# Two transpose groups per slot, and a small network's first layer moved into the runs of value products

## The chip, the cores and the metric

The kernel runs on one core of a Trainium2 chip. TensorE (PE in the profile) multiplies matrices, with its weight loads shown apart as PEld; VectorE (DVE), ScalarE (ACT) and GpSimd (POOL) work element by element; SyncE (SP) issues most of the DMA transfers. The metric is the device time of one launch in microseconds (us), the median of several runs. Before the change it is 2571.12 us (2569.76 to 2571.41 in three runs).

## The reference

Two layers on 512 rows of 1024 floats. Each layer is: a gated feed-forward block, a token mixer, a second feed-forward block, each followed by a layer norm. All time of interest here is in the token mixer:

```python
q_a, kv_a, g_a, q_b, k_b, v_b, q_c, k_c, v_c, f_c = _split_cols(h @ w_in)
o_a = _nsa(...)        # branch a: compressed + selected + window keys, gated
o_b = _swa_sink(...)   # branch b: window of 128, with a sink
o_c = _fox(...)        # branch c: causal, with a forget gate
merged = g[:, :, 0] * (o_a @ w_br_a) + g[:, :, 1] * (o_b @ w_br_b) + g[:, :, 2] * (o_c @ w_br_c)
return merged @ w_out
```

Branch a compresses its keys and values first. Blocks of 32 positions of 64 numbers, flattened to 2048, go through a small network of two layers, `gelu(flat @ w1) @ w2`, with a hidden size of 256; there is one such network for keys and one for values. The first layer, `flat @ w1`, is the "compressed branch's first layer" of this text: sixteen steps (k = 0 to 15) of 128 of the 2048 inputs each, for keys and for values.

## The kernel before, in words

**Products.** Operands of the projections are split in two halves of the fp32r type, a high and a low one (`wsplit`, lines 140 and 141: ScalarE rounds, VectorE subtracts). A product is three matmuls of 512 columns (`mm3`, lines 161 to 163: high by high, low by high, high by low).

**The fill queue.** In the mixer, a projection of 128 columns of `w_in` is a `chunk`: eight closures of three matmuls each, appended to the queue `fill`. The first closure takes the weights and a PSUM tile of the tag `mm`; the last hands the finished tile to a function that moves it out (`set_q` with `ev_q`, lines 403 and 404; `ev_k`, lines 421 and 422; `ev_z`, lines 502 to 510). `pump(n)` runs n closures. A closure wrapped in `free` counts for nothing. So the order of the chunks in the code is the order in which the projections become ready.

**Attention.** `batches` lists the work: eight pairs of branch-b units (`Swa`), then, for each of four pairs of heads, three batches of branch-c and branch-a units (`Fox`, `Nsa`). `step(cur, prev, n)` is one step of a software pipeline. It issues the score products of the batch `cur` (generator `s`: products, then bias, maximum, exponential and norm on VectorE, ScalarE and GpSimd) and the transposes of the batch `prev` (generator `tr`), spread over `slots` with closures of the fill queue between them. Then it issues the value products of `prev` (`pv`, into one PSUM tile of the tag `po`), and moves them out (line 1019). `PUMPS` has the number of closures for each step. If a batch needs a projection that isn't ready, `need` pumps until it is.

**Transposes.** One call of `next(it)` yields one group: one to four 128x128 transposes into a PSUM tile of the tag `tp` (lines 641, 692, 793, 799), which `ev_pt` copies back (line 395 on ScalarE, line 393 on VectorE). The tag has two buffers. So has `mm`; `sc`, for scores, has three, and `po` one.

**The small network.** `conv` gives eight `part` closures. Each loads two steps k of both networks into a buffer of the weights' ring `raw` (line 532, two DMAs of 256 KB) and issues four matmuls (line 536) into one PSUM tile `hid`: keys to partitions 0 to 63, values to 64 to 127. The parts are dealt out among the closures of the fill queue. After the last part comes the gelu, then `tr` (two transposes into a `tp` tile, `glT`), then `conv2`, the second layer.

**Order.** TensorE and GpSimd issue in the order of the code (`manual_schedule`); the order on VectorE, ScalarE and SyncE is made by the framework's scheduler, at build time, from its own estimate of when things are ready. PSUM and SBUF buffers of a tag are also given out at build time.

Of the kernel before, what the change touches and what calls it, by code (L numbers as in the profile page):

```python
# [18 lines left out]
P = 128  # L19
# [45 lines left out]
def body(tc, a, out, depth=DEPTH):  # L65
# [47 lines left out]
    def wraw(shape=None):  # L113
        return wt.tile(list(shape or [P, KD, P]), F32, name="raw", tag="raw", bufs=3)
# [237 lines left out]
    def mix(l, wts, pend, done_ffn, xap, xa, nxt):  # L352
# [161 lines left out]
        def conv(ws):  # L514


            c = K()
            c.wk = at.tile([P, 2, 2, DH], F32, name="cw2k", tag="p", bufs=PB)
            c.wv = at.tile([P, 2, DH], F32, name="cw2v", tag="p", bufs=PB)
            v = a["cmp_k_w2"][l].rearrange("(c p) d -> p c d", p=P)  # L520
            for r in range(2):
                nc.sync.dma_start(c.wk[:, :, r], v)
            nc.sync.dma_start(c.wv, a["cmp_v_w2"][l].rearrange("(c p) d -> p c d", p=P))
            wv = [w.rearrange("(c p) f -> p c f", p=P) for w in ws]

            def part(j):
                def go():
                    if j == 0:
                        c.p = ps("sc", "hid", (P, 256))
                    r = wraw([P, 2, 2, 256])  # L530
                    for i in range(2):
                        nc.sync.dma_start(r[:, i], wv[i][:, 2 * j:2 * j + 2])
                    for k in (2 * j, 2 * j + 1):
                        for i in range(2):
                            z = (m.zk, m.zv)[i][k // 8][:, k % 8].rearrange("p g n -> p (g n)")
                            nc.tensor.matmul(c.p[64 * i:64 * i + 64], z, r[:, i, k % 2], start=k == 0, stop=k == 15)
                    if j == 7:
                        x = at.tile([P, 2, 256], F32, name="gl", tag="p", bufs=PB)
                        t, c.t = x[:, 0], x[:, 1]
                        nc.scalar.activation(t, c.p, AF.Square)  # L540
                        nc.vector.tensor_scalar(t, t, 0.044715, 1.0, op0=OP.mult, op1=OP.add)
                        nc.vector.tensor_tensor(t, t, c.p, op=OP.mult)
                        nc.scalar.activation(t, t, AF.Tanh, scale=GELU_C)
                        nc.vector.scalar_tensor_tensor(c.t, t, 1.0, c.p, op0=OP.add, op1=OP.mult)
                return go

            def tr():
                pt = ps("tp", "glT", (P, 2, P))
                for f in range(2):
                    nc.tensor.transpose(pt[:, f], c.t[:, f * P:(f + 1) * P], ident)  # L550
                x = at.tile([P, 3, P], F32, name="glt", tag="p", bufs=PB)
                c.gk = x[:, 0].rearrange("p (f n) -> p f n", f=2)
                c.gv = x[:, 1:3].rearrange("p f (g r n) -> p f g r n", g=2, r=2)
                nc.vector.tensor_copy(c.gk, pt[:, :, 0:64])
                for f in range(2):
                    nc.vector.tensor_copy(c.gv[:, f], pt[:, f, 64:P].rearrange("p (g n) -> p g n", g=2)[:, :, None]
                                          .to_broadcast([P, 2, 2, NSLOT]))

            return c, [part(j) for j in range(8)], tr

        def conv2(c):

# [35 lines left out]
        class Swa:  # L598
# [37 lines left out]
            def tr(u):  # L636
                pv = u.p.rearrange("p s (b q) -> p s b q", q=P)[:, :, 0:u.nb]
                pt = ps("tp", "ptS", (P, 2, 2, P))[:, :, 0:u.nb]
                for s in range(2):
                    for b in range(u.nb):  # L640
                        nc.tensor.transpose(pt[:, s, b], pv[:, s, b], ident)
                ev_pt(pv, pt, 4)
                yield
# [170 lines left out]


        fill = deque()
        FREE = "free"

        def free(f):
# [5 lines left out]
        def wgf():  # L825

            r = wraw()
            v = w_in.rearrange("(k p) f -> p k f", p=P)
            nc.sync.dma_start(r[:, :, 0:24], v[:, :, CGA:CGA + 24])
            nc.sync.dma_start(r[:, :, 24:32], v[:, :, CFC:CFC + 8])  # L830
            w = wt.tile([P, KD, P], F32R, name="hi", tag="hi", bufs=3)
            nc.scalar.activation(w[:, :, 0:32], r[:, :, 0:32], AF.Copy)
            nc.vector.tensor_tensor(w[:, :, 32:64], r[:, :, 0:32], w[:, :, 0:32].bitcast(F32), op=OP.subtract)
            return w, None

        def chunk(c0, then, w=w_in, load=wcols):
            st = K()

            def part(i):
                def go():  # L840
                    if i == 0:
                        st.w = load(w, c0)
                        st.p = ps("mm", "pj")
                    proj(st.p, st.w, ks=range(i, i + 1))
                    if i == 7:
                        then(st.p)
                return go

            fill.extend(part(i) for i in range(8))

        def set_q(lst, i):
            def go(p):
                t = ev_q(p)
                fill.insert(min(4, len(fill)), free(lambda: lst.__setitem__(i, t)))
            return go
# [36 lines left out]
        def nsa_k(b):  # L892
            def go(p):
                if not m.ka:
                    for g in range(2):
                        m.ka[g] = (ks_tile(), ks_tile())
                dst = lambda g: tuple(t.rearrange("p (k b) j -> p k b j", b=2)[:, :, b] for t in m.ka[g])
                ev_k(p, dst)
            return go

        def pump(n=1):
            while n > 0 and fill:
                n -= fill.popleft()() is not FREE

# [12 lines left out]
        chunk(CKB, set_kb)  # L917
        chunk(CQB, set_q(m.qb, 0))
        chunk(0, set_gf, load=lambda w, c0: wgf())
        chunk(CQB + P, set_q(m.qb, 1))  # L920
        pump(29)
        chunk(CKV + 0, lambda p: setattr(m, "zk", ev_z(p, 0)))
        chunk(CQB + 2 * P, set_q(m.qb, 2))
        chunk(CKV + P, lambda p: setattr(m, "zv", ev_z(p, 1)))
        fill.append(lambda: m.cum())
        cv, parts, tr = conv([a["cmp_k_w1"][l], a["cmp_v_w1"][l]])
        n0 = len(fill)
        chunk(CQB + 3 * P, set_q(m.qb, 3))
        fox_chunks(0)
        rest = [fill.pop() for _ in range(len(fill) - n0)][::-1]  # L930
        for i, f in enumerate(rest):
            fill.append(f)
            if i >= 6 and parts:
                fill.append(parts.pop(0))
        fill.append(tr)
        chunk(CKV + 2 * P, nsa_k(0))
        fill.append(lambda: conv2(cv))
        chunk(CKV + 4 * P, nsa_k(1))
        chunk(CQA, set_q(m.qa, 0))
        fox_chunks(1)  # L940
        chunk(CQA + P, set_q(m.qa, 1))
        fox_chunks(2)
# [38 lines left out]
        def step(cur, prev, n):  # L981


            for u in cur:
                while not need(u):
                    pump(1)
                    n -= 1
            it, iu = chain(u.tr() for u in prev), chain(u.s() for u in cur)
            nt, ns = sum(u.ngrp for u in prev), sum(u.nseg for u in cur)
            slots = max(nt, ns, 1)  # L990
            done = 0

            def upto(x):
                nonlocal done
                x = int(round(x))
                if x > done:
                    pump(x - done)
                    done = x

            last = min(2, max(n, 0))  # L1000
            n -= last
            for j in range(slots):
                if j * ns // slots != (j + 1) * ns // slots or slots == ns:
                    next(iu, None)
                upto(n * (2 * j + 1) / (2 * slots))
                if j * nt // slots != (j + 1) * nt // slots or slots == nt:
                    next(it, None)
                upto(n * (j + 1) / slots)
            for _ in iu:
                pass  # L1010
            for _ in it:
                pass
            pump(last)
            if prev:
                po = ps("po", "po", (P, 4, P))
                for j, u in enumerate(prev):
                    u.pv(po[:, j])
                for j, u in enumerate(prev):
                    nc.scalar.activation(o_t[u.br][u.m][:, u.qb * P:(u.qb + 1) * P], po[:, j], AF.Copy)

        PUMPS = [11] * 5 + [12] * 3 + [11, 10, 11] * 4 + [8]
        for cur, prev, n in zip(batches + [[]], [[]] + batches, PUMPS):
            step(cur, prev, n)
        while fill:
# [197 lines left out]
```

## Time and profile before

| | |
|---|---|
| median of three runs | 2571.12 us (2569.76 to 2571.41) |
| the profiled execution | 2569.58 us, its span 2567.9 us |
| TensorE busy | 2549.1 us (99%) |
| VectorE, ScalarE, GpSimd busy | 1197.6, 950.1 and 177.5 us |
| granted TensorE clock, mean | 0.998 |
| attention of the first and the second layer | about 417 to 717 and 1690 to 1990 us of the span |

A row of a timeline has the start, the time from the start to the last end, the engine, the line, and what was written from what, with a count where equal neighbours are merged; a bracket holds the idle time before it and what ended it. Matmuls overlap in the pipeline: a row of 0.39 us that is followed by the next one 0.23 us later has cost 0.23 us. So prices on TensorE are read here from start to start. An fp32 matmul that is not a transpose stands in the trace as two; the transposes, and the fp32r products, as one. A row of a group has the busy time, the mean of one in ns, and after the bar the idle time of its engine before it.

### The profile page before, as it was taken

How to read it: one execution, taken by the hardware profiler on the slowest of the kernel's cores; microseconds unless marked ns; L12 is line 12 of the kernel's file. 1: busy time of each engine (PE TensorE's matmuls, PEld its weight loads, DVE VectorE, ACT ScalarE, POOL GpSimd, SP SyncE). 2: the span in 40 equal slices, each digit the busy share in tenths (PEclk: the TensorE clock that was granted, in tenths of full speed). 3: DMA queues.
4: the chain of work that ended last, by engine and by line, in shares of the span. 5: the costliest groups of instructions: out<-in, count | busy, mean ns of one | idle time of the engine just before them, and what ended most of it. 6: DMA issues, size and time to landing. Idle time of an engine off the chain costs nothing.

```text
span 2567.9 us, 34023 instructions
## 1 busy us (share of the span) xinstructions
PE 2549.1 (99%) x13099; PEld 2104.2 (82%) x13099; DVE 1197.6 (47%) x2563; ACT 950.1 (37%) x1949; POOL 177.5 (7%) x371
## 2 busy tenths in 40 slices
PE   9999999999999999999999999999999999999998
PEld 8888887788888888888888888877888888888887
DVE  4344245676654354332343432555766534544323
ACT  3222134477642332222232221345776323322211
POOL 0000000133300000000000000101332000000000
PEclk9999999999999999999999999999999999999999
DMA  6433333633143333333333333426321434233331
GB/s 214 117 93 97 99 93 112 180 91 83 50 143 99 119 102 96 99 99 93 113 91 98 93 97 99 121 77 190 90 82 41 145 101 148 81 93 98 99 93 63
DMA packets 374658, 268.97 MB, mean 105 GB/s; under 512 B 16872, under 2 KB 350760, under 8 KB 374496
## 3 DMA queue, kind: packets, MB, share of 16 engines
q1 hardware_dynamic: 373344, 262.61, 35.1%
q0 software_dynamic: 1152, 4.19, 0.4%
q8 instruction: 103, 1.69, 0.3%
q14 instruction: 59, 0.48, 0.1%
HBM read 247.83 MB, written 9.49 MB: 100 GB/s over the span
## 4 chain that ended last, share of the span: by engine, by line
PE 95%; DVE 2%; DMA 1%; ACT 1%; issue 1%; POOL 0%; DVEq 0%; POOLq 0%; ACTq 0%
PE acc L175 7%; PE acc L174 7%; PE acc L176 7%; PE pg L161 6%; PE pg L163 6%; PE pg L162 6%; PE pu L161 6%; PE pu L163 6%; PE pu L162 6%; PE pj L161 5%; PE pj L163 5%; PE pj L162 5%; PE gate L161 3%; PE gate L162 3%; PE gate L163 3%; PE brp L162 2%
## 5 line engine op out<-in xcount | busy, mean ns | idle before, releaser
L141 DVE TENSOR_TENSOR lo<-raw,hi 128x1024 fp32r<-128x1024 f32 (+2 forms) x414 | 490.8, 1189 | 856.1 <-ACT hi L140 854.5
L140 ACT ACTIVATE hi<-raw 128x1024 fp32r<-128x1024 f32 (+2 forms) x414 | 424.6, 1031 | 1225.3 <-issue 695.9
L161 PE MATMUL pj<-xh,hi 128*128 128x512 f32 (+1 forms) x720 | 272.6, 379 | 2.6 <-ACT vt L448 1.4
L163 PE MATMUL pj<-xh,lo 128*128 128x512 f32 (+1 forms) x720 | 255.5, 355 | 0.7 <-DVE lo L141 0.5
L162 PE MATMUL pj<-xl,hi 128*128 128x512 f32 (+1 forms) x720 | 254.5, 353 | 0.1
L162 PE MATMUL pg<-xl,hi 128*128 128x512 f32 x640 | 249.7, 390 | 0.0
L163 PE MATMUL pg<-xh,lo 128*128 128x512 f32 x640 | 249.7, 390 | 0.0
L161 PE MATMUL pg<-xh,hi 128*128 128x512 f32 x640 | 249.6, 390 | 0.0
L163 PE MATMUL pu<-xh,lo 128*128 128x512 f32 x640 | 249.0, 389 | 0.0
L161 PE MATMUL pu<-xh,hi 128*128 128x512 f32 x640 | 249.0, 389 | 0.0
L162 PE MATMUL pu<-xl,hi 128*128 128x512 f32 x640 | 249.0, 389 | 0.0
L174 PE MATMUL acc<-hi,ha 128*128 128x512 f32 x576 | 227.3, 395 | 0.0
L175 PE MATMUL acc<-hi,ha 128*128 128x512 f32 x576 | 227.3, 395 | 0.0
L176 PE MATMUL acc<-lo,ha 128*128 128x512 f32 x576 | 227.2, 395 | 0.0
L286 DVE TENSOR_TENSOR t<-t,pu 128x512 f32<-128x512 f32 x80 | 55.0, 687 | 216.3 <-PE pu L163 216.3
L161 PEld LDWEIGHTS pj<-xh,hi 128*128 128x128 f32 x720 | 136.5, 190 | 22.0 <-issue 6.6
L163 PEld LDWEIGHTS pj<-xh,lo 128*128 128x128 f32 x720 | 135.5, 188 | 21.6 <-DVE lo L141 1.8
L162 PEld LDWEIGHTS pj<-xl,hi 128*128 128x128 f32 x720 | 136.5, 190 | 9.8 <-DVE xl L221 0.4
L163 PEld LDWEIGHTS pg<-xh,lo 128*128 128x128 f32 x640 | 120.5, 188 | 25.3
L161 PEld LDWEIGHTS pg<-xh,hi 128*128 128x128 f32 x640 | 120.6, 188 | 24.9
L162 PEld LDWEIGHTS pg<-xl,hi 128*128 128x128 f32 x640 | 120.3, 188 | 25.0
L162 PEld LDWEIGHTS pu<-xl,hi 128*128 128x128 f32 x640 | 120.2, 188 | 25.0
(243 smaller groups left out, 4223.3 us busy)
## 6 DMA issues: line engine op xcount, KB each, us to landing
raw<-in_ffn_w_dram SPq DMA_DIRECT2D x264, 512.0 KB, 3.8
raw<-in_w_in_dram SPq DMA_DIRECT2D x56, 512.0 KB, 4.0
raw<-in_w_gate_dram SPq DMA_DIRECT2D x48, 512.0 KB, 3.9
ks<-hl SPq DMA_DIRECT2D x96, 128.0 KB, 2.5
raw<-in_w_out_dram SPq DMA_DIRECT2D x16, 512.0 KB, 3.6
tab<-bvec SPq DMA_DIRECT2D x16, 256.0 KB, 3.0
x_sp<-xa POOLq DMA_DIRECT2D x8, 512.0 KB, 7.4
raw<-in_cmp_k_w_dram SPq DMA_DIRECT2D x16, 256.0 KB, 3.3
```

Of the source, the lines that this page charges most:

```text
L140: nc.scalar.activation(hi[:, c], raw[:, c], AF.Copy)
L141: nc.vector.tensor_tensor(lo[:, c], raw[:, c], hi[:, c].bitcast(F32), op=OP.subtract)
L161: nc.tensor.matmul(o, hi[:, k], vh, start=first, stop=False)
L162: nc.tensor.matmul(o, hi[:, k], vl, start=False, stop=False)
L163: nc.tensor.matmul(o, lo[:, k], vh, start=False, stop=last)
L174: nc.tensor.matmul(o, sh(k)[:, t], hi[:, c], start=k == 0, stop=False)
L175: nc.tensor.matmul(o, sl(k)[:, t], hi[:, c], start=False, stop=False)
L176: nc.tensor.matmul(o, sh(k)[:, t], lo[:, c], start=False, stop=k == nk - 1)
L286: nc.vector.tensor_tensor(t, t, pu, op=OP.mult)
```

## The change

Three things change, all within the mixer.

1. `step` issues transposes two groups at a time: the number of groups is halved for the spreading over slots, and each time `next(it)` is called twice in a row.
2. The small network's first layer goes in single steps k, not in parts of two. `feed` issues the two loads of one step (128 KB each), into a tile of the tag `p` (13 buffers, used by the attention's probabilities too) and no longer into the weights' ring; up to four may wait. Its products are kept in a queue, `narrow`, and `step` runs all that wait there right after the value products of `prev`, before these are moved out. `feed` stands in the fill queue ahead of each closure of the chunks behind it, as a `free` one. `end` runs what is left, and then `tr`. The two tiles of second-layer weights become one.
3. The chunks are put in another order, so that the network's inputs (`zk`, `zv`) come before the second and third query chunk of branch b; the first `pump` runs 32 closures, not 29; `tr` and `conv2` stand later in the queue; and `PUMPS` has 11 closures fewer, since the parts are gone from the queue.

```diff
             c = K()
-            c.wk = at.tile([P, 2, 2, DH], F32, name="cw2k", tag="p", bufs=PB)
-            c.wv = at.tile([P, 2, DH], F32, name="cw2v", tag="p", bufs=PB)
+            w2 = at.tile([P, 2, 3, DH], F32, name="cw2", tag="p", bufs=PB)
+            c.wk, c.wv = w2[:, :, 0:2], w2[:, :, 2]
...
-            def part(j):
+            def load(k):
+                r = at.tile([P, 2, 256], F32, name="cw1", tag="p", bufs=PB)
+                for i in range(2):
+                    nc.sync.dma_start(r[:, i], wv[i][:, k])
+
                 def go():
-                    if j == 0:
+                    if k == 0:
                         c.p = ps("sc", "hid", (P, 256))
-                    r = wraw([P, 2, 2, 256])
                     for i in range(2):
-                        nc.sync.dma_start(r[:, i], wv[i][:, 2 * j:2 * j + 2])
-                    for k in (2 * j, 2 * j + 1):
-                        for i in range(2):
-                            z = (m.zk, m.zv)[i][k // 8][:, k % 8].rearrange("p g n -> p (g n)")
-                            nc.tensor.matmul(c.p[64 * i:64 * i + 64], z, r[:, i, k % 2], start=k == 0, stop=k == 15)
-                    if j == 7:
+                        z = (m.zk, m.zv)[i][k // 8][:, k % 8].rearrange("p g n -> p (g n)")
+                        nc.tensor.matmul(c.p[64 * i:64 * i + 64], z, r[:, i], start=k == 0, stop=k == 15)
+                    if k == 15:
...
-            return c, [part(j) for j in range(8)], tr
+            c.n = 0
+
+            def feed():
+
+                if c.n < 16 and len(narrow) < 4:
+                    narrow.append(load(c.n))
+                    c.n += 1
+
+            def end():
+                while narrow or c.n < 16:
+                    feed()
+                    narrow.popleft()()
+                tr()
+
+            return c, feed, end
...
+        chunk(CKV + 0, lambda p: setattr(m, "zk", ev_z(p, 0)))
+        pump(32)
+        chunk(CKV + P, lambda p: setattr(m, "zv", ev_z(p, 1)))
         chunk(CQB + P, set_q(m.qb, 1))
-        pump(29)
-        chunk(CKV + 0, lambda p: setattr(m, "zk", ev_z(p, 0)))
+        cv, feed, tr = conv([a["cmp_k_w1"][l], a["cmp_v_w1"][l]])
+        n0 = len(fill)
         chunk(CQB + 2 * P, set_q(m.qb, 2))
-        chunk(CKV + P, lambda p: setattr(m, "zv", ev_z(p, 1)))
         fill.append(lambda: m.cum())
-        cv, parts, tr = conv([a["cmp_k_w1"][l], a["cmp_v_w1"][l]])
-        n0 = len(fill)
         chunk(CQB + 3 * P, set_q(m.qb, 3))
         fox_chunks(0)
         rest = [fill.pop() for _ in range(len(fill) - n0)][::-1]
-        for i, f in enumerate(rest):
+        for f in rest:
+            fill.append(free(feed))
             fill.append(f)
-            if i >= 6 and parts:
-                fill.append(parts.pop(0))
+        chunk(CKV + 2 * P, nsa_k(0))
+        chunk(CKV + 4 * P, nsa_k(1))
         fill.append(tr)
-        chunk(CKV + 2 * P, nsa_k(0))
-        fill.append(lambda: conv2(cv))
-        chunk(CKV + 4 * P, nsa_k(1))
         chunk(CQA, set_q(m.qa, 0))
+        fill.insert(len(fill) - 2, lambda: conv2(cv))
...
             nt, ns = sum(u.ngrp for u in prev), sum(u.nseg for u in cur)
+            pair = 2
+            nt = (nt + pair - 1) // pair
...
-                    next(it, None)
+                    for _ in range(pair):
+                        next(it, None)
...
                 for j, u in enumerate(prev):
                     u.pv(po[:, j])
+                while narrow:
+                    narrow.popleft()()
...
-        PUMPS = [11] * 5 + [12] * 3 + [11, 10, 11] * 4 + [8]
+        PUMPS = [10] * 8 + [11, 10, 11] * 4 + [8]
```

More of the change, by code (lines that the diff above doesn't have):

```diff
@@ L816, in mix @@
         fill = deque()
+        narrow = deque()
         FREE = "free"
```

## The prediction, as put on record before the changed kernel had run

> **What bounds the kernel now.** I read the page first, then the windows by stage, then TensorE's waits within the attention, then its timeline there.
>
> ```profile
> span 2567.9 us, 34023 instructions
> PE 2549.1 (99%) x13099; PEld 2104.2 (82%) x13099; DVE 1197.6 (47%) x2563; ACT 950.1 (37%) x1949; POOL 177.5 (7%) x371
> ...
> PE 95%; DVE 2%; DMA 1%; ACT 1%; issue 1%; POOL 0%; DVEq 0%; POOLq 0%; ACTq 0%
> ...
> 417.00:717.00 300.00, 297.36 (x2041) 238.98 (x2040) 202.03 (x787) 196.89 (x619) 74.70 (x151) 1.00 0.36 99
> ```
>
> TensorE is busy 99% of the span and 95% of the chain that ended last. The last row is the attention of the first layer (columns: busy time of PE, PEld, DVE, ACT, POOL, then clock and DMA): TensorE idles 2.6 us of 300. So a change here gains only by making TensorE's own instructions cheaper, or by ending one of its few waits; and it loses by any new wait, since nothing behind TensorE can absorb one. These are its waits in that window (us in total, times, longest):
>
> ```profile
> PE ptC L799 <- ACT p L395: 0.7, 1, 0.7
> PE pj L161 <- ACT vt L448: 0.7, 1, 0.7
> PE pj L161 <- DVE qs L404: 0.6, 1, 0.6
> PE ptF L692 <- DVE pc L393: 0.3, 1, 0.3
> PE po L649 <- DVE p L393: 0.2, 1, 0.2
> ```
>
> The second layer's attention shows the same five. All others are below a tenth.
>
> **First part: the small network's products.** One of the eight parts before, alone among fp32r products:
>
> ```profile
> 463.44 0.40 PE L163 MATMUL pj<-xh,lo 128*128 128x512 f32 x1
> 463.77 1.08 PE L536 MATMUL hid<-raw,z 128*64 128x256 f32 x8
> 464.79 0.50 PE L161 MATMUL pj<-xh,hi 128*128 128x512 f32 x1
> 465.12 0.39 PE L162 MATMUL pj<-xl,hi 128*128 128x512 f32 x1
> 465.35 0.40 PE L163 MATMUL pj<-xh,lo 128*128 128x512 f32 x1
> ...
> L536 PE MATMUL hid<-raw,z 128*64 128x256 f32 x128 | 17.3, 392 | 0.0
> ```
>
> From 463.44 to 465.12 are 1.68 us. Two ordinary steps (465.12 to 465.35: 0.23) would take 0.46, so the part costs 1.22. Its eight matmuls go in pairs, one to each half of the columns: the row's 1.08 less the last one's own 0.39 (mean of this line) leaves 0.69 for three steps from pair to pair, 0.23 each, 0.94 for four with rounding. The other 0.28 is for going into 64-column matmuls (0.33 from 463.44, not 0.23) and out of them (0.33 behind 464.79, and the rest at the last pair). The value products have the same 64-column form, so the network's products behind them pay no entry and no exit of their own. In the issue order of the changed kernel (built, not run) all sixteen steps stand in five of the runs of value products (3, 4, 4, 4 and 1), and no part stands alone. Gain: 8 x 0.28 = 2.25 us a layer.
>
> The Trainium skill (TensorEngine Tiling, section Tiling Modes, Key Properties) says that a change of tiling mode drains the engine, a change of tile does not. By it the gain is the same 2.25 a layer here, and pairing transposes, which are full 128x128 operations as the fp32r products are, gains nothing at all; the sum by the rule is 0.4 us above mine for both layers.
>
> **Second part: pairs of transposes on TensorE.** One group of one transpose and one of four:
>
> ```profile
> 669.11 0.39 PE L163 MATMUL pj<-xh,lo 128*128 128x512 f32 x1
> 669.34 0.27 PE L692 MATMUL ptF<-ident,p 128*128 128x128 f32 x1
> ...
> 669.68 0.39 PE L162 MATMUL pj<-xl,hi 128*128 128x512 f32 x1
> ...
> 640.07 0.39 PE L163 MATMUL pj<-xh,lo 128*128 128x512 f32 x1
> 640.30 0.60 PE L793 MATMUL ptN<-ident,p 128*128 128x128 f32 x4
> ...
> 640.97 0.39 PE L162 MATMUL pj<-xl,hi 128*128 128x512 f32 x1
> ```
>
> The first takes 0.57 from L163 to L162, so 0.11 beyond the two ordinary steps; the second 0.90, so 0.44, 0.11 for each transpose. There is no price for beginning or ending a run: at most 0.01, the rounding. The issue order has 47 runs fewer a layer, worth 0 to 0.47 us. I take 0.2.
>
> **Third part: the waits that come.** A group's tile is one of two `tp` banks, so a group waits until the group that had the bank has been copied out. That this copy can come late is seen before the change:
>
> ```profile
> 565.16 0.60 PE L793 MATMUL ptN<-ident,p 128*128 128x128 f32 x4
> ...
> 567.67 0.40 PE L163 MATMUL pj<-xh,lo 128*128 128x512 f32 x1
> 568.80 0.30 PE L799 MATMUL ptC<-ident,pc 128*128 128x128 f32 x1 [0.73 <-ACT p L395]
> ...
> 566.26 1.05 ACT L140 ACTIVATE hi<-raw 128x1024 fp32r<-128x1024 f32 x1
> 567.21 0.58 ACT L403 ACTIVATE qs<-pj 64x512 fp32r<-64x512 f32 x1
> 567.68 0.40 ACT L766 ACTIVATE p<-p,stN 128x128 f32<-128x128 f32 x1
> 568.07 0.58 ACT L395 ACTIVATE p<-ptN 128x512 f32<-128x512 f32 x1
> ```
>
> The group of 565.16 is ready at 565.76 and copied at 568.07 to 568.65, behind a weight split, a query copy and an exponential that stand ahead of it in ScalarE's fixed order. The next user of the bank starts at 568.80, 1.13 us behind 567.67 where 0.23 is ordinary: a cost of 0.90, more than the bracket's 0.73. The order on ScalarE is fixed at build time, so for the changed kernel I went through it group by group, with durations of these rows:
>
> ```profile
> L140 ACT ACTIVATE hi<-raw 128x1024 fp32r<-128x1024 f32 (+2 forms) x414 | 424.6, 1031 | 1225.3 <-issue 695.9 <-PE acc L175 295.6 <-DMA raw<-in_ffn_w_dram 55.7
> L395 ACT ACTIVATE p<-ptS 128x512 f32<-128x512 f32 (+1 forms) x24 | 12.4, 518 | 10.1 <-PE ptS L641 9.6
> L393 DVE COPY p<-ptS 128x512 f32<-128x512 f32 x8 | 5.5, 683 | 3.5 <-PE ptS L641 2.8 <-POOL p L596 0.7
> L403 ACT ACTIVATE qs<-pj 64x512 fp32r<-64x512 f32 x48 | 28.2, 587 | 9.9 <-DVE qs L404 7.5 <-PE pj L163 2.0
> L404 DVE SCALAR_TENSOR_TENSOR qs<-pj,qs 64x512 fp32r<-64x512 f32 x48 | 33.1, 689 | 6.7 <-ACT qs L403 5.2
> L628 ACT ACTIVATE p<-p,stS 128x256 f32<-128x256 f32 (+1 forms) x64 | 30.3, 475 | 31.4 <-DVE stS L624 31.4
> ...
> 445.06 0.88 PE L649 MATMUL po<-p,v 128*64 128x128 f32 x12
> 445.87 0.66 PE L615 MATMUL sS<-ks,qs 128*128 128x128 f32 x4
> ```
>
> - *Second query chunk of branch b, 1.5 us.* It now stands behind both `z` chunks, and the third step's first scores (batch `Swa(1, 0)`) need it. From its end, ScalarE has a weight split (1.0), a query half (0.5, a start-to-start value like the next ones), four exponentials (0.5 each), small ones and two copies of `po` (0.6, an estimate), the other half (0.5), then VectorE the last quarter (0.7): 5.3, and some 0.6 in which ScalarE waits for the scores' maxima. TensorE has three closures (0.69 each), the value products (445.06 to 445.87: 0.8) and three narrow steps (six pairs, 1.4) until then: 4.3, with an entry. Wait: 5.9 - 4.3, about 1.5 (0 if ScalarE gains 1.5 us there; 2.2 at most by these rows).
> - *One pair in one bank, 0.8 us.* The tile of the cumulative sum still holds the other bank, so in the fourth step both groups of a pair have the same one: the second starts when the first is copied (0.52, and 0.3 from the last transpose to the copy's start).
> - *The network's `tr` right behind a pair, 1.0 us.* Its tile has the bank of the pair's second group, with nothing between: 0.68 for that copy on VectorE and 0.3 to its start.
> - *First step with a mixed batch, 0.5 us,* a pair's first copy behind a split and a key copy.
> - *The place of 568.80, 1.5 us.* Both groups of the next pair now wait, where the 0.90 was: the first 0.7, as the bracket has it, the second for one more exponential and copy (0.39 and 0.5) less its neighbour's transpose (0.1), 0.8.
> - *One mixed step later, 1.6 us.* ScalarE's order there is split, exponential, query half, two exponentials, copy. The rows 566.26 to 568.65 have the same with two exponentials fewer, 2.4 us; with 0.39 more for each (567.68 to 568.07) 3.2. TensorE has between the two pairs only two score products of two matmuls (0.24 each), one closure (0.77) and one transpose (0.1), some 1.4, and the split starts some 0.2 before the first pair ends.
> - *The other pairs:* none by the same count, or 0.1 to 0.2 each; 0.9 together.
>
> Together 7.8 us a layer. Bounds: 0 (all copies in time), and 11 (each 40% more, as the place of 568.80 came out 0.90 where counting by the rows gives 0.7).
>
> **Fourth part: the waits that go.** Of the five waits, the one on `vt` stays, as it lies ahead of the change. The others (0.7, 0.6, 0.3, 0.2) go or are replaced by those above; read from start to start they cost some 0.15 more each: 2.4 us a layer.
>
> **Fifth part: loads and queues.**
>
> ```profile
> 434.16 0.37 SPq L532 DMA_DIRECT2D raw<-in_cmp_k_w_dram  x1
> 434.58 0.46 SPq L532 DMA_DIRECT2D raw<-in_cmp_v_w_dram  x1
> ...
> ks<-hl SPq DMA_DIRECT2D x96, 128.0 KB, 2.5
> ...
> raw<-in_cmp_k_w_dram SPq DMA_DIRECT2D x16, 256.0 KB, 3.3
> ```
>
> SyncE issues 16 loads more a layer, 6.7 us of its queue in some 55. They wait for buffers of the tag `p`, and weight loads and bias tables stand behind them. After a run all four narrow buffers are free at once: eight issues of 0.42 and 3.3 to land are 6.7 us, and the next run is a step (9 us or more) away. The first run is closest: six issues behind a weight load, 2.5 us, and 3.3 to land, some 1 us before the third narrow step. I take 0; this cover gone, it costs what lands late, up to 3 us a layer. The 16 weight-ring buffers given free are worth nothing: no wait for weights is among the five. The later `tr` and `conv2` cost only the 1.0 above: the first Nsa scores come three steps behind.
>
> The Trainium skill (DMA: Bandwidth & Descriptors, section Bandwidth, its Rule) says that small transfers should be batched; halving them goes against it. By its fit of 2 us and the bytes, an estimate, a load of 128 KB would take 2.3 us, and the wait stays 0.
>
> **Sum.** A layer: + 7.8 - 2.4 - 2.25 - 0.2 = + 2.95; both layers + 5.8 us. The profiled execution took 2569.58, 1.7 more than its span, so 2575.4; the median of the runs shown is 1.5 above it: **2576.9 us**. What the measurement can tell from no change is about 0.2%, 5.1 us, so this is slower, and barely.
>
> **The rivals.**
> - *Copies in time, faster.* If ScalarE runs earlier than I count, the new waits shrink, and the gains of 2.45 and 2.4 remain. It decides at 4.85 us of waits a layer: below, the kernel is faster. With 1.5 to 2 us left: 2571.1 - 6 = 2565. For it: the order is made by a scheduler that had the copies ahead; against it: the order is fixed, and the same scheduler left the 0.90.
> - *Half of the waits, no change.* 5 us a layer: 2571. For it: three of the six rest on counts of 1.5 us between two engines.
> - *Narrow loads late, slower still.* In the first run, behind a weight load that itself waits for a ring buffer; 3 us a layer more: 2583. The margin of 1 us speaks against it.
> - *The products cost the same in a run.* Then 4.5 us are not gained: 2581. Against it: the entry and exit of the row at 463.44.
>
> **How the numbers follow.** Forecast with most of the waits, 2573.5 to 2581: 0.53 (0.09 of it within 0.2%). Copies in time: 0.20 (0.02 within). Half the waits: 0.18 (0.03 faster). Late loads: 0.06, products as dear: 0.03. So faster 0.21, the same 0.26, slower 0.53. The range of 8 in 10 takes in the faster rival's 2565 and the late loads' 2583.
>
> **What would show it.** Right: no `hid` row alone among `pj` rows, the 0.28 gone with each; more idle time of TensorE in both attention windows, some 5 us each; waits of the score line of Swa on `qs` L404, of `glT`, and of `ptS`, `ptC` and `ptN` on the copies of L395 and L393. Wrong: TensorE's waits in these windows stay at 2.5 us, or a wait of `hid` on `cw1`.

## The result, and the profile after

| | median | runs | profiled span |
|---|---|---|---|
| before, beside it | 2570.97 us | 8 (2568.58 to 2571.97) | 2567.9 us |
| changed kernel | 2576.93 us | 8 (2576.58 to 2580.93) | 2575.0 us |

The ratio is 1.0029, with a 95% interval of 1.0018 to 1.0040: slower by 6.0 us, and by more than the 0.2% that can be told from no change. The forecast was 2576.9.

The page of the changed kernel, and its windows of the two attentions (columns as in the prediction):

```profile
span 2575.0 us, 34112 instructions
PE 2544.7 (99%) x13099; PEld 2109.3 (82%) x13099; DVE 1197.1 (46%) x2565; ACT 949.3 (37%) x1947; POOL 184.4 (7%) x371
...
417.00:719.50 302.50, 294.03 (x2035) 240.23 (x2034) 200.76 (x786) 195.33 (x616) 78.22 (x151) 1.00 0.36 98
719.50:1692.00 972.50, 972.36 (x4496) 809.78 (x4495) 395.20 (x490) 277.79 (x354) 13.91 (x29) 1.00 0.35 104
1692.00:1995.00 303.00, 294.51 (x2037) 240.88 (x2036) 200.81 (x788) 195.37 (x616) 78.08 (x151) 1.00 0.36 98
```

TensorE is busy 4.4 us less than before (2549.1 to 2544.7), and the span is 7.1 us longer. TensorE now idles 8.5 us in each attention, where it idled 2.6; between the two it idles 0.1 us of 972. So the change shortens TensorE's own work, as it was meant to, and pays more in waits. These are TensorE's waits in the first attention (us in total, times, longest); the second shows the same, within 0.1 us:

```profile
PE ptN L807 <- ACT p L395: 2.9, 4, 1.6
PE sS L629 <- DVE qs L404: 1.3, 1, 1.3
PE glT L550 <- DVE p L393: 0.9, 1, 0.9
PE ptS L655 <- DVE p L610: 0.9, 1, 0.9
PE ptS L655 <- ACT p L395: 0.8, 1, 0.8
PE ptC L813 <- ACT p L395: 0.7, 1, 0.7
PE pj L161 <- ACT vt L448: 0.7, 1, 0.7
PE ptS L655 <- POOL z L500: 0.2, 1, 0.2
```

All of them but two were in the prediction. The two are `ptS` behind `p` L610 on VectorE and, right after it, behind GpSimd, which makes the other half of this norm (from 442.26 for 0.94 us; the row names the memset that comes next there). Here they are in the timelines of TensorE and VectorE:

```profile
441.40 0.38 PE L655 MATMUL ptS<-ident,p 128*128 128x128 f32 x2
442.63 0.41 PE L655 MATMUL ptS<-ident,p 128*128 128x128 f32 x2 [0.85 <-DVE p L610]
443.25 0.44 PE L655 MATMUL ptS<-ident,p 128*128 128x128 f32 x2 [0.22 <-POOL z L500]
...
432.01 2.35 DVE L510 TENSOR_TENSOR z<-vt,peT 64x248 f32<-64x248 f32 x4
...
434.67 2.41 DVE L508 TENSOR_TENSOR z<-vt,peT 64x256 f32<-64x256 f32 x4
437.09 0.42 DVE L605 CUSTOM_DVE_ANT_0 p<-sS,tab 128x256 f32<-128x256 f32 x1
...
439.35 2.35 DVE L510 TENSOR_TENSOR z<-vt,peT 64x248 f32<-64x248 f32 x4
441.73 0.16 DVE L644 TENSOR_TENSOR stS<-stS 128x2 f32<-128x2 f32 x1
...
442.13 0.35 DVE L610 TENSOR_SCALAR p<-p,stS 128x256 f32<-128x256 f32 x1
```

The second group needs the norm of its unit (L610). This unit's maxima (437.09) stand behind the eight additions for the first `z` chunk (432.01 to 437.08), and its norm behind four for the second (2.35 us). Before, VectorE had this unit's maxima and norm out of the way ahead of the first addition:

```profile
432.06 0.42 DVE L591 CUSTOM_DVE_ANT_0 p<-sS,tab 128x256 f32<-128x256 f32 x1
...
437.11 0.35 DVE L596 TENSOR_SCALAR p<-p,stS 128x256 f32<-128x256 f32 x1
...
439.75 2.34 DVE L510 TENSOR_TENSOR z<-vt,peT 64x248 f32<-64x248 f32 x4
```

Below, the cost of a wait is read from start to start, against the median of the same sequence of matmuls in the profiles of all kernels of this study. It is 0.1 to 0.2 above the bracket.

### The profile page after: what moved, and what is told of

Its sections match the earlier page's. It is cut to its first block, busy times and chain, and to the rows that moved or that the text cites. A ratio compares the mean times of both kernels' runs of the same rounds, so it can differ in the third digit from the quotient of the medians.

```text
span 2575.0 us, 34112 instructions
## 1 busy us (share of the span) xinstructions
PE 2544.7 (99%) x13099; PEld 2109.3 (82%) x13099; DVE 1197.1 (46%) x2565; ACT 949.3 (37%) x1947; POOL 184.4 (7%) x371
## 5 line engine op out<-in xcount | busy, mean ns | idle before, releaser
L161 PE MATMUL pj<-xh,hi 128*128 128x512 f32 (+1 forms) x720 | 267.2, 371 | 1.5 <-ACT vt L448 1.4
L203 POOL TENSOR_SCALAR st<-st 128x1 f32<-128x1 f32 x24 | 8.4, 352 | 1890.4 <-ACT junk L201 1890.4
```

What stands on the lines that cost most here:

```text
L161: nc.tensor.matmul(o, hi[:, k], vh, start=first, stop=False)
L203: nc.gpsimd.tensor_scalar(st[:, 4:5], st[:, 3:4], 1.0 / D, EPS / ALPHA ** 2, op0=OP.mult, op1=OP.add)
```

## The experiments

Theory 1, from the prediction: the pairs make waits, since the copies that free the two `tp` banks stand late in the order of ScalarE and VectorE; the narrow products gain. Theory 2: the pairs are neutral, and the moved chunks, the loads and the additions for `z` cost the time. Kernels that share a value of before ran on one chip beside it.

| kernel | median, us | before there | ratio to before, 95% interval |
|---|---|---|---|
| narrow products alone | 2568.29 | 2569.79 | 0.9991 (0.9982 to 1.0000) |
| pairs alone | 2580.28 | 2569.79 | 1.0037 (1.0024 to 1.0050) |
| changed, pairs in branch b only | 2571.63 | 2569.79 | 1.0006 (0.9997 to 1.0015) |
| changed, pairs in mixed batches only | 2575.08 | 2569.79 | 1.0018 (1.0009 to 1.0027) |
| narrow, query chunk first | 2578.11 | 2569.74 | 1.0036 (1.0023 to 1.0049) |
| narrow, loads fed a chunk earlier | 2565.27 | 2569.74 | 0.9984 (0.9975 to 0.9994) |
| narrow, half of the additions for `z` | 2568.57 | 2569.74 | 0.9995 (0.9985 to 1.0004) |
| changed, copies on VectorE | 2578.52 | 2569.74 | 1.0039 (1.0025 to 1.0053) |
| changed, two tiles moved | 2575.17 | 2570.57 | 1.0016 (1.0007 to 1.0026) |
| loads earlier, more copies on VectorE | 2565.31 | 2570.57 | 0.9981 (0.9972 to 0.9990) |

### The two parts apart

The narrow part alone:

```diff
-            pair = 2
+            pair = 1
```

> One part alone: the network's narrow products and the new order of the chunks, with transposes in single groups. Theory 1 (the pairs of transposes cost the time, the narrow products gain it): TensorE's work gets about 5.4 us shorter, as in the changed kernel. Of the waits that came with the change only the first scores' wait on the second query chunk stays (some 1.4 us a layer); the old waits on ptC (0.9) and ptF (0.5) are back, those of the two pj rows (0.7 and 0.4) and of po are gone. Together about 5.5 us less than before: 2565.5, and not over 2569. Theory 2 (the pairs are neutral; the moved chunks, the loads and the additions of z cost the time): no better than the changed kernel, 2575 to 2578.

Measured: 2568.29, 1.5 us below before where 5.5 was expected, and its interval reaches no change. Its waits in the first attention:

```profile
PE sS L629 <- DVE qs L404: 1.3, 1, 1.3
PE ptS L655 <- DVE p L610: 0.8, 1, 0.8
PE ptC L813 <- ACT p L395: 0.7, 1, 0.7
PE pj L161 <- ACT vt L448: 0.7, 1, 0.7
PE ptF L706 <- DVE pc L393: 0.3, 1, 0.3
PE ptS L655 <- POOL p L610: 0.2, 1, 0.2
PE po L663 <- DVE p L393: 0.2, 1, 0.2
```

Theory 2 falls as to its size: this is not the changed kernel's time. But theory 1 is not whole either. TensorE's work got 5.4 us shorter, as expected; 3.5 us of it went back in waits, because the `ptS` wait on the norm (1.35 us a layer) stays without any pair. It belongs to the moved chunks.

The pairs alone, in the kernel before:

```diff
             nt, ns = sum(u.ngrp for u in prev), sum(u.nseg for u in cur)
+            pair = 2
+            nt = (nt + pair - 1) // pair
...
-                    next(it, None)
+                    for _ in range(pair):
+                        next(it, None)
```

> The other part alone: the kernel before, with the transposes two groups at a time and nothing else. Theory 1: TensorE's work stays within 0.5 us of before (a run of transposes costs nothing to begin or to end), and the waits on the two tp banks come as in the changed kernel: ptN 1.8, 0.7, 0.6 and 0.5, ptS 1.0 a layer, less ptF 0.5 and 0.2 that go: some 4 us a layer, 2579 in all (2577 to 2581). Theory 2: 2571, as before.

Measured: 2580.28, 10.5 us above before, more than the 8 expected. By the interval (6 to 13 us) the two are not told apart; the trace has more waits than expected. Read from start to start, TensorE's work is 0.5 us shorter and its waits in the two attentions 10.2 us longer. (Its busy time is 0.4 us longer, 2549.5 against 2549.1: a bracket holds 0.1 to 0.2 us less than the wait costs, and the rest counts as busy.) All the expected waits are there with the expected sizes; beyond them came `ptS` with 0.84 in the first attention and 0.25 in the second, and this one, in the timelines of TensorE and VectorE:

```profile
460.50 0.66 PE L649 MATMUL po<-p,v 128*64 128x128 f32 x8 [1.20 <-DVE p L393]
...
458.08 1.76 DVE L508 TENSOR_TENSOR z<-vt,peT 64x256 f32<-64x256 f32 x3
459.77 0.68 DVE L393 COPY p<-ptS 128x512 f32<-128x512 f32 x1
```

The copy of a pair's second group stands behind the additions for `z`, here in the old order of chunks. That the value products catch up with it because the pair comes later in its step is argued, not tested.

### Where the pairs cost it

```diff
-            pair = 2
+            pair = 2 if all(u.br == 1 for u in prev) else 1
```

> The changed kernel with pairs only where the batch of the transposes is one of branch b (the first eight steps). Theory 1: against the narrow part alone it adds the ptS wait of two groups in one bank (1.0), the wait of glT (1.0) and that of ptS for norm and z (1.4), a layer: 3.4 at most, 1.8 if the last is not the pairs' own. So 3.6 to 6.8 us above the narrow part alone, 2569 to 2572.5. Theory 2: the same time as the changed kernel and as the narrow part alone.

```diff
-            pair = 2
+            pair = 1 if all(u.br == 1 for u in prev) else 2
```

> The changed kernel with pairs only in the mixed batches (branches a and c). Theory 1: against the narrow part alone it adds the ptN waits of 1.8, 0.7, 0.6 and 0.5 a layer, and takes away the ptF waits of 0.5 and 0.2: some 2.9 us a layer, 5.8 in all, 2571.5; what this kernel and the one with pairs in branch b alone add to the narrow part makes up what the changed kernel adds to it (11 us). Theory 2: the same time as the changed kernel and as the narrow part alone.

Measured: 2571.63 and 2575.08. The second is 3.6 us above the expected 2571.5, 2.8 of it because the narrow part alone is that much above its own expectation. The two are 3.3 and 6.8 us above the narrow part alone, 10.1 together, against 7.5 by the medians of the changed kernel and of the narrow part (each against its own before), and 9.2 by their profiled spans. In the first attention the waits are 1.6 us above the narrow part with pairs in branch b (`ptS` 1.00 and `glT` 1.02, less 0.33 of `po`), and 3.4 with pairs in the mixed batches (`ptN` 1.80, 0.67, 0.61 and 0.51, less two of `ptF`). The `ptS` wait on the norm is in both, so it isn't the pairs' own. Some two thirds of the pairs' price are the mixed batches'.

### Why the copies are late: the engine's order, or two banks

```diff
-                if n and eng[0] % n == 0:
+                if True:
                     nc.vector.tensor_copy(dst, src)
```

> The changed kernel with every copy of a transposed group on VectorE. Theory 1 (the second group of a pair waits because the copies of the groups before stand in ScalarE's order behind splits, query halves and exponentials): the waits of ptN and ptC on ScalarE (2.9 and 0.7 a layer) go down to 0.5 together, while those for VectorE grow: ptS 1.4, and scores, whose maxima now stand behind copies, some 1.9 in the mixed steps. In all within 3 us of the changed kernel. Theory 2 (two banks for two groups at a time make the wait, whichever engine copies): ptN and ptC wait for VectorE as long as they did for ScalarE.

Measured: 2578.52, above the changed kernel by 1.6 us by the medians and 2.6 by the ratios (1.0039 against 1.0029), with intervals that overlap. Some of its waits in the first attention:

```profile
PE ptS L655 <- DVE vt L489: 1.5, 1, 1.5
PE sN L765 <- DVE stN L605: 0.9, 1, 0.9
...
PE sN L765 <- DVE stF L605: 0.8, 1, 0.8
...
PE ptN L807 <- DVE p L393: 0.4, 1, 0.4
```

The 1.8, 0.84 and 0.67 us of `ptN` and `ptC` are gone, so two banks alone don't make those waits: the place in ScalarE's order does. But VectorE's order is as tight. The scores now wait for maxima (L605) that stand behind copies.

Two waits could be taken away by small moves in the changed kernel:

```diff
-        fill.append(lambda: m.cum())
         chunk(CQB + 3 * P, set_q(m.qb, 3))
+        fill.append(lambda: m.cum())
...
-        fill.append(tr)
         chunk(CQA, set_q(m.qa, 0))
+        fill.insert(len(fill) - 6, tr)
```

> The changed kernel with two small moves and nothing else: the cumulative sum is issued a chunk later, so that its tile no longer holds one of the two tp banks while the pair of the fourth step is transposed, and the network's tr comes two closures later. Theory 1 (each wait has its own place: the same bank for both groups of one pair; a tile right behind a pair): ptS 1.0 (the one for ScalarE) and glT 1.0 go, all other waits stay: 4 us in all below the changed kernel, 2573. Theory 2 (the copies are late as a whole, so a wait that goes comes back at the next group): the same 2577, with new waits of ptS or ptF in these steps.

Measured: 2575.17; by the ratios (1.0016 against 1.0029) 3.3 us below the changed kernel, by the medians 1.8, and the intervals overlap. At an equal mean clock the difference is plainer: three runs at 0.999 average 2572.0 us, three of the changed kernel 2576.9, and 4 us less was expected. In the trace both waits are gone and none came in their place: the first attention waits 9.6 us in all, where the changed kernel waits 11.7. The second shows 11.0, as TensorE's clock fell there for a while (last section). So these waits are separate: one that goes doesn't come back at the next group.

### The waits of the moved chunks

The cause of the `ptS` wait on the norm was tested in the narrow part alone by leaving work out: `z` has one tile in place of two, so the second half of the additions isn't made and its products use the first tile again.

```diff
-            z = [at.tile([P, 8, 2, NSLOT], F32, name="z", tag="p", bufs=PB) for _ in range(2)]
-            nc.gpsimd.memset(z[1][:, :, :, NSLOT - 1:NSLOT], 0.0)
+            z = [at.tile([P, 8, 2, NSLOT], F32, name="z", tag="p", bufs=PB)] * 2
...
-                    nc.vector.tensor_tensor(z[1][o, :, g, 0:NSLOT - 1], pv[:, half, :, 1:NSLOT],
-                                            pe[:, 1][:, :, None].to_broadcast([64, 8, NSLOT - 1]), op=OP.add)
```

> The narrow part with single groups, half of the additions for z left out: z has one tile, used for all sixteen steps, in place of two, so VectorE has eight additions fewer a layer (0.58 us each) and TensorE the same products. Theory 1 (the wait of ptS on the norm is the time that VectorE needs for the four additions ahead of it): ptS waits 0 to 0.3 a layer, not 1.4; sS keeps its 1.6, since the query halves stand behind exponentials. So 2 to 3 us below the narrow part alone, 2565.8. Theory 2 (the norm is late for ScalarE's exponentials or for GpSimd): ptS waits as before, 2568.

Measured: the wait is gone from the trace (the group starts at 441.06 with no idle time before it), and `sS` waits twice, 1.04 and 1.07, so 2.1 in all and not 1.64. The profiled span is 2563.6, 2.2 below the narrow part alone, as expected; the median of ten runs, 2568.57, is not below it. Among runs with the same mean clock it is: at 0.998 six runs average 2567.0 and four of the narrow part alone 2568.9, at 0.997 two average 2568.8 and two 2570.3.

```profile
438.22 2.39 DVE L507 TENSOR_TENSOR z<-vt,peT 64x256 f32<-64x256 f32 x4
...
441.06 0.60 PE L652 MATMUL ptS<-ident,p 128*128 128x128 f32 x4
```

With fewer additions VectorE's order is another one, too: the norm starts at 436.53, no longer at 442.14, and so ahead of the second chunk's additions (438.22). So it is shown that the additions ahead of maxima and norm make the wait; what each of them costs is not.

The other one, `sS` for the second query chunk:

```diff
-        chunk(CKV + P, lambda p: setattr(m, "zv", ev_z(p, 1)))
-        chunk(CQB + P, set_q(m.qb, 1))
         cv, feed, tr = conv([a["cmp_k_w1"][l], a["cmp_v_w1"][l]])
         n0 = len(fill)
+        chunk(CKV + P, lambda p: setattr(m, "zv", ev_z(p, 1)))
+        chunk(CQB + P, set_q(m.qb, 1))
...
-                while narrow:
+                while narrow and hasattr(m, "zv"):
```

(with `pair = 1`, as all that follow but those called "changed" in the table)

> The narrow part with single groups and the changed order of chunks; only the loads of the narrow steps start a chunk earlier (four of them, so the first run has four steps and not three), which also gives ScalarE and VectorE another order at this place: both halves of the second query chunk stand ahead of two exponentials and of two maxima. Theory 1: the wait of sS on qs falls from 1.6 to 0.1 or 0.2 a layer, that of ptS on the norm (1.4) stays: 3 us below the narrow part alone, 2565.5, and 4 us below before. Theory 2 (sS waits for qs because TensorE finishes the chunk too late, not for the order of the two engines behind it): 2568, as the narrow part alone.

Measured: 2565.27, 4.5 us below before and outside the interval of no change. The waits of the first attention:

```profile
PE ptS L655 <- DVE p L610: 0.9, 1, 0.9
...
PE sS L629 <- DVE qs L404: 0.4, 1, 0.4
```

`sS` waits 0.58 where it waited 1.64 (0.1 to 0.2 was expected). The query's second half is issued on ScalarE ahead of two exponentials, at 447.70 and no longer at 449.02, while TensorE is only 0.26 us earlier there (its value products start at 446.14, not 446.40). So the order behind the chunk, not the chunk, was late. It isn't all of the gain, though: of the 1.06 us that went, 0.43 is the fourth narrow step, which TensorE now does in that time.

With the query chunk back ahead of `z`:

```diff
+        chunk(CQB + P, set_q(m.qb, 1))
+        pump(32)
         chunk(CKV + 0, lambda p: setattr(m, "zk", ev_z(p, 0)))
-        pump(32)
         chunk(CKV + P, lambda p: setattr(m, "zv", ev_z(p, 1)))
-        chunk(CQB + P, set_q(m.qb, 1))
```

> The narrow part with single groups, but the second query chunk of branch b put back ahead of both z chunks. Theory 1 (VectorE holds back the norm and the query's last quarter, since sixteen additions for z stand ahead of them): the waits of ptS on the norm (1.4 a layer) and of sS on qs (1.6) go; the narrow steps come as early as before while z comes a chunk later, so hid waits for z or for its loads, about 5 a layer: 2 x (5 - 3) = 4 to 5 us above the narrow part alone, 2573. Theory 2 (z and the loads are in time anyway, and the order of the chunks alone is dear): no wait of hid, 6 us below the narrow part alone, 2562.

Measured: 2578.11, 5 us more than theory 1 said. Both waits are gone, and TensorE's first narrow run shows what came:

```profile
449.12 0.62 PE L536 MATMUL hid<-cw,z 128*64 128x256 f32 x2 [2.01 <-DMA cw<-in_cmp_k_w_dram]
453.63 2.82 PE L536 MATMUL hid<-cw,z 128*64 128x256 f32 x10 [3.89 <-DVE z L508]
```

First a load is late (the first is issued at 446.34, in the changed kernel at 439.88), then `z`; and in this gap the clock fell (last section). The order of chunks in the change is what keeps both on time.

Last, the kernel with loads earlier and `ev_pt(p, pt, 2)` in place of `ev_pt(p, pt, 3)` for branch a:

> The kernel with single groups and loads fed a chunk earlier, and, of the copies of branch a's groups, every second and not every third on VectorE. Theory 1 (what is left of the waits is the place of single copies in ScalarE's order): ptC's 0.9 a layer goes, at most 0.4 of ptF comes, 1 us in all below that kernel: 2564.5. Theory 2 (VectorE's order is as tight): the same 2565.3 or up to 1 us more.

Measured: 2565.31 (ratio 0.9981). `ptC` waits 0.16 in place of 0.89, and `ptF` 0.35 and `ptC` 0.22 came elsewhere; 0.5 us of waits less in both attentions together by the trace, which the runs can't tell from none. This and the kernel with loads earlier beat both kernels; their intervals lie below 1.

## Why the prediction was right, point by point

| step, us a layer | predicted | measured in the first attention |
|---|---|---|
| network's products | - 2.25 | - 2.7 |
| fewer runs of transposes | - 0.2 | - 0.25 to - 0.3 |
| `sS`, second query chunk | + 1.5 | + 1.67 |
| one pair in one bank | + 0.8 | + 1.00 |
| `tr` behind a pair | + 1.0 | + 1.02 |
| first mixed step | + 0.5 | + 0.51 |
| place of 568.80 | + 1.5 | + 0.84 and 0.67 |
| one mixed step later | + 1.6 | + 1.80 |
| other pairs | + 0.9 | + 0.61 and 0.15 |
| `ptS` behind norm and `z` | not seen | + 1.01 and 0.38 |
| old waits that go | - 2.4 | - 3.2 |

The sum of the right column is + 3.5 a layer, 7.0 in both; the spans differ by 7.1 and the medians by 6.0. The predicted one was + 2.95 a layer, which makes 5.9 for both (the prediction says 5.8).

- *First part.* The mechanism was right, the size 0.5 too small. In the changed kernel's timeline, beside the rows at 445.06 and 445.87 of before:

```profile
473.28 0.88 PE L663 MATMUL po<-p,v 128*64 128x128 f32 x12
473.99 1.90 PE L536 MATMUL hid<-cw,z 128*64 128x256 f32 x16
475.82 0.66 PE L629 MATMUL sS<-ks,qs 128*128 128x128 f32 x4
```

From the value products to the scores are 2.54 us, where before they were 0.81: 1.73 for four steps, 0.43 each. Before, a step cost 0.61. Sixteen times 0.18 is 2.9; TensorE's work in the narrow part alone fell by 2.7 a layer. The prediction had taken 0.47 a step. The rival in which the products cost the same in a run is out.

- *Second part.* A run of transposes costs next to nothing to begin or to end. The pairs alone shorten TensorE's work, from start to start, by 0.5 us in both layers, and so do they on top of the narrow part.

The Trainium skill (TensorEngine Tiling, section Tiling Modes, Key Properties) has a drain at a change of tiling mode and none at a change of tile. By that rule the products gain and the pairs gain nothing. The trace agrees on the first (0.61 to 0.43 a step), and nearly on the second (0.01 a run for the 47 runs).

- *Third part.* Each counted wait came where it was put, within 0.2 us. What is missing is the group at 442.63, which waits 1.39, and which waits without any pair as well. The prediction used that `z` now comes ahead of the query chunk, but not that the first `z` chunk is now done before the attention begins (it stands ahead of the first `pump`, of 32 closures), so that its additions on VectorE meet the first units' maxima and norms. They had no term in the sum. That the additions are the cause is shown by the kernel that leaves half of them out.
- *Fourth part.* All but the wait on `vt` went, and the smaller ones that had been left out of the count (0.1 to 0.4 each, from start to start) went too: 0.8 more.
- *Fifth part.* No `hid` waits for a load in the changed kernel, though the loads land later than taken:

```profile
cw<-in_cmp_k_w_dram SPq DMA_DIRECT2D x32, 128.0 KB, 3.5
```

The 2.3 us that the prediction works out by the fit of the Trainium skill (DMA: Bandwidth & Descriptors, section Anatomy of one DMA) is shorter still; the page states this fit for transfers that GpSimd issues, and these are issued by SyncE. The rival of late loads was a near one: with one chunk moved, a load was 2.0 us late.

The two misses (waits of 1.4 that were not seen, gains of 0.5 and 0.8 that were too small) nearly cancel, and that is luck. So the total is closer than its terms. That 2576.93 meets 2576.9 is luck too: the prediction put the median 1.5 us above the profiled execution, which took 2576.70 and not 2575.4.

## What to carry to other kernels

On an engine that is busy 99%, a change of issue order is priced by what stands ahead of each producer on the other engines; go through every engine that feeds the moved work, not only the ones the change speaks of. Apart, the two parts of this change have opposite signs, so a bundle is worth taking apart: its good half, fed a little earlier, beat the kernel before. A wait that comes with pairing can sit in one place and be moved away there, without coming back at the next group.

## What the runs showed of the hardware

A wait can cost more than its length. In the kernel with two tiles moved, TensorE waits 0.85, 0.22, and 1.33 us in the second attention within nine microseconds, and then:

```profile
1726.32 0.44 PE L629 MATMUL sS<-ks,qs 128*128 128x128 f32 x2 [1.33 <-DVE qs L404]
...
1727.34 0.57 PE L161 MATMUL pj<-xh,hi 128*128 128x512 f32 x1
1727.70 0.63 PE L162 MATMUL pj<-xl,hi 128*128 128x512 f32 x1
1728.13 0.63 PE L163 MATMUL pj<-xh,lo 128*128 128x512 f32 x1
...
1730.69 0.46 PE L163 MATMUL pj<-xh,lo 128*128 128x512 f32 x1
...
1723.00:1726.50 3.50, 2.08 (x20) 1.18 (x16) 3.06 (x8) 2.50 (x11) 1.36 (x3) 1.00 0.68 175
1726.50:1730.50 4.00, 4.00 (x13) 3.23 (x14) 1.45 (x9) 0.97 (x5) 0.52 (x2) 0.61 0.96 304
```

For some 3.4 us the granted clock is half, a step takes 0.43 and not 0.23, and eight steps (1727.34 to 1730.69) cost 1.5 us more, as much as the wait itself. The same place has the same waits in the first attention of that kernel and in both of the changed kernel, at full clock; the kernel with pairs in mixed batches has the fall in the second attention only, the one with all copies on VectorE in the first only. In the kernel with the query chunk first the clock falls within the gap of 3.9 us, which follows one of 2.0, and is half for over five microseconds:

```profile
449.00:453.60 4.60, 0.62 (x2) 0.19 (x2) 4.48 (x8) 1.00 (x3) 1.36 (x3) 0.80 0.39 123
453.60:456.40 2.80, 2.77 (x11) 1.25 (x11) 1.22 (x1) 0.00 (x0) 0.00 (x0) 0.50 0.10 25
456.40:459.00 2.60, 2.60 (x10) 2.31 (x10) 0.83 (x6) 0.57 (x3) 0.00 (x0) 0.58 1.10 332
```

Where it falls is seen in profiled executions only, but each run's mean granted clock is known to a thousandth, and it goes with the spread of the runs (2565.3 to 2570.5 with the narrow part alone). There, five runs at 0.999 average 2566.4 us, four at 0.998 2568.9 and two at 0.997 2570.3; with two tiles moved, three at 0.999 average 2572.0, five at 0.998 2575.2 and two at 0.997 2576.8. With the `sS` wait shortened, where the runs lie within 2.1 us, 0.999 and 0.998 average the same.

The Trainium skill (TensorE: Matmul & The Clock Gate, section Part 1: The HAM clock gate) has the clock at half after at least one idle window of about 3.4 us, and the windows run freely. The trace agrees on the half clock and on 3.4 us, and that the same waits bring a fall in one place and not in another would fit windows that run freely. An idle window of that length did not come before every fall, though: no gap before the one at 1727.34 was over 1.5 us.
